# A decoder layer on one core: two row buffers serve first as weight tiles and then as a store for eight more expert results

## The chip, the cores and the metric

The kernel runs on one core of one Trainium2 chip. The metric is the device time of one execution in microseconds (us). Engines are named as in the profile: PE is TensorE's matmul side (PEld its weight loads), DVE is VectorE, ACT is ScalarE, POOL is GpSimd, SP is SyncE, which here only issues DMAs.

## The reference, cut to what matters

One decoder layer over 512 tokens of width 1024, in float32. A token sublayer (retention, forgetting attention, branch gates, projections) is followed by a layer norm. The channel sublayer is where the change lies:

```
def peer(x, w_q, sub_keys, expert_u, expert_v):         # per block of 128 tokens
    q = (xc @ w_q).reshape(n, HEADS, 2, HALF)
    sc = einsum('nhcd,hckd->nhck', q, sub_keys)
    s, idx = top_k(sc, 16)                              # per half key
    cand = s[..., 0, :, None] + s[..., 1, None, :]      # 16 x 16 sums per head
    top_s, pos = top_k(cand, 16);  eid = cid[pos]       # 8 heads x 16 experts of 16384
    gate = softmax(top_s)
    hid = einsum('nhkd,nd->nhk', expert_u[eid], xc)
    act = gelu(hid) * gate
    return einsum('nhk,nhkd->nd', act, expert_v[eid])
h <- LN(alpha*h + peer(h) + sigmoid(h @ W_g + b_g) * (p @ W_ple))
```

## The kernel before, in words

The 512 tokens are two groups of two blocks of 128. Both groups pass through the token sublayer, the first group first. In the channel sublayer they are treated in two ways.

**First group, by gathering.** For each of its two blocks GpSimd gathers 128 rows of `peer_u` and 128 rows of `peer_v` per token partition, one row of 512 KB (128 partitions by 1024 floats) per indirect DMA (`Gather.fetch`, L1081). DVE multiplies a u row with the token and sums it (L1087), and adds a v row, weighted, to the residual (L1097). These 512 row steps run on DVE and in the DMA queues beside everything else, from about 385 us on. Six row buffers (`ROWS`) hold them, and two more (`MORE`) from the beginning of the last stage on.

**Second group, densely.** All 16384 experts are run for its 256 tokens, in 128 steps of 128 experts:
- `up(b)`: eight float32 matmuls of 128x256 (tile `hid`, 16 records in the profile) and a Gelu on ACT into a tile `a`. Weights `ur` come as 1 MB for two steps.
- a gate `gw` per expert and token, which is made from the routing (`select`, on DVE; tile `rt` holds its result) by one-hot products: `by_slot` turns `rt` (matmuls `gt`), DVE writes one-hot tiles `oa` and `ob`, PE multiplies them (`gp`), and ACT copies the products to staging tiles, which go to DRAM (`spread`). There are two spreads, one per block, each 16 pairs of `oa` and `ob`.
- `down(b)`: twelve fp32r matmuls of 128x512 into four PSUM tiles `acc`, from `a` times gate split in high and low parts (`ah`, `al`) and from `peer_v` split likewise (`vh` on ACT, `vl` on DVE).

The gate must be complete before the first `down`, but an `up` needs only the tokens. So 44 ups (`lead`) run early, as filling between other work of PE, and 4 more (`RES`) in the `acc` tiles at the beginning of the last stage. Their results wait in SBUF in the pool `ap`, 50 tiles (`lead + RES + XTRA`). In the last stage the other 80 ups are dealt out between the 128 downs.

**What sets the order.** DVE, POOL and PE run in the order in which the program is written (`in_order`); ACT and SP are ordered by the compiler's scheduler. The written order comes from a planner, `Clock`: it adds estimated times of PE, DVE and the DMA queues. `rows()` puts a row step into DVE's order where the estimate of DVE lies behind that of PE, and `k.fill` puts an up into PE's order, at most 8 at a time, where DVE's estimate is more than 2 us ahead of PE's. Four ups (`RES`) are always left to be issued after the second spread.

**Weight tiles.** `load_raw` (L325) loads projection weights as tiles `wr` of 512 KB into three buffers `wraw` that are used in turn. SP issues the load of a tile when the tile three before it has been used up.

Of the kernel before, what the change touches and what calls it, by code (L numbers as in the profile page):

```python
# [9 lines left out]
F32 = mybir.dt.float32  # L10
# [7 lines left out]
S, D, P = 512, 1024, 128  # L18
# [3 lines left out]
HEADS, K, NK = 8, 16, 128  # L22
# [109 lines left out]
class Clock:  # L132
# [3 lines left out]
    base, more = 0.07, 0.06  # L136
# [72 lines left out]
def setup(ctx, tc, I):  # L209
    k = Ctx()  # L210
    k.clock = Clock()
    nc = Core(tc.nc, k.clock)
    k.nc, k.tc, k.I = nc, tc, I
    k.cp = ctx.enter_context(tc.tile_pool(name="cp", bufs=1))
    k.fp = ctx.enter_context(tc.tile_pool(name="fp", bufs=1))
    k.wp = ctx.enter_context(tc.tile_pool(name="wp", bufs=3))
    k.dr = ctx.enter_context(tc.tile_pool(name="dr", bufs=1, space=DRAM))
    k.tp = None
    k.n = 0
    k.feed, k.side, k.slow, k.fill = Feed(), Feed(), Feed(), Feed()  # L220
    k.later = []

    def flush():

        while k.later:
            f, *a = k.later.pop(0)
            f(*a)

    def rows():
        while k.feed.items and k.clock.row():  # L230
            k.feed.step()

    def tick():
        due, k.later = k.later, []
        for f, *a in due:
            f(*a)
        k.side()
        k.slow()
        k.fill()
        rows()  # L240
    k.tick, k.flush, k.clock.before = tick, flush, rows

    def slot(shape, dt, tag, name):
        pool = k.cp if tag in ("S1", "S2", "S3") else k.q1
        return pool.tile(shape, dt, tag=tag, name=name)
    k.slot = slot

    def uniq(s):
        k.n += 1
        return f"{s}_{k.n}"  # L250
    k.uniq = uniq
    return k
# [71 lines left out]

def load_raw(k, src, c2, g):  # L325

    raw = k.wp.tile([P, 2, 512], F32, tag="wraw", name=k.uniq("wr"))
    k.nc.sync.dma_start(raw, src[g, c2])
    return raw

# [652 lines left out]
ROWS, MORE = 6, 2  # L983
XTRA = 2
RES = 4


class Experts:
# [7 lines left out]
    def up(self, b, ps=None):  # L996
        k, nc, ND = self.k, self.k.nc, self.ND
        if b % 2 == 0:
            self.uraw = k.us.tile([P, 2, 8, P], F32, tag="uraw", name=k.uniq("ur"))
            nc.sync.dma_start(self.uraw, k.I["uT"][b // 2])  # L1000
        if ps is None:
            ps = self.ph.tile([P, ND], F32, tag="hid", name=k.uniq("hid"))
        for c in range(8):
            nc.tensor.matmul(ps, self.uraw[:, b % 2, c, :], k.h1[:, c, :], start=c == 0, stop=c == 7)
        a = self.ap.tile([P, ND], F32, tag="a", bufs=self.lead + RES + XTRA, name=k.uniq("a"))
        nc.scalar.activation(a, ps, AF.Gelu)
        self.act[b] = a

# [91 lines left out]
def channel(k, dense, lead, ctx):  # L1100
    nc, tc, I = k.nc, k.tc, k.I
# [2 lines left out]
    k.us = ctx.enter_context(tc.tile_pool(name="us", bufs=2))  # L1104
    ph = ctx.enter_context(tc.tile_pool(name="ph", bufs=2, space=PSUM))
    ex = Experts(k, dense, gd, lead, ap, ph)
    k.fill.items, k.fill.rate = [(ex.up, b) for b in range(lead)], 8
    k.fill.when = lambda: len(k.fill.items) > RES and k.clock.dve > k.clock.pe + 2
    k.clock.pace, k.clock.due, k.clock.base, k.clock.more = 4.2, k.clock.pe, 0.085, 0.115
    c0 = ExitStack()  # L1110
    with ExitStack() as c1:
        k.pp = c1.enter_context(tc.tile_pool(name="pp2", bufs=4, space=PSUM))
        k.px = c1.enter_context(tc.tile_pool(name="px2", bufs=2, space=PSUM))
        rp = c0.enter_context(tc.tile_pool(name="rp", bufs=2, side="right"))
        routed = [[rp.tile([P, HEADS * K], F32, bufs=1, name=f"rt{n}_{i}") for i in range(3)] for n in range(2)]
        with ExitStack() as c2:
            kp = c2.enter_context(tc.tile_pool(name="kp", bufs=2))
            s16, i16 = product_keys(k, REST, rp, kp, k.h1)
            k.side.items, k.side.rate = [select(k, rp, s16[:, 0], i16[:, 0], *routed[0])], 2.25
            embedding_gate(k, REST, k.h1, kp)  # L1120
            k.side.drain()
        with ExitStack() as c2:
            sps = [c2.enter_context(tc.tile_pool(name=f"sp{i}", bufs=1)) for i in range(2)]
            k.obs = k.slot([P, 2, 8, P], F32, "S2", "ob")
            tabs = k.fp.tile([P, 8, P], F32, tag="xg", bufs=FIRST.nt, name="tabs")
            k.iota = tabs[:, 6, :]
            nc.sync.dma_start(k.iota, I["iota"])
            k.side.items, k.side.rate = [select(k, rp, s16[:, 1], i16[:, 1], *routed[1])], 0.65
            for n in range(len(dense)):
                k.fill()  # L1130
                tr = tabs[:, 3 * n:3 * n + 3, :]
                by_slot(k, tr, routed[n])
                if n == len(dense) - 1:
                    c0.close()
                    dv = ctx.enter_context(tc.tile_pool(name="dv", bufs=2, side="right"))
                    for b in (0, 2):
                        ex.fetch(b, dv)
                for i, _ in enumerate(spread(k, sps, tr, n * P, gd, 4 if n else 8)):
                    k.clock.hold = n == len(dense) - 1 and i >= 28
                    k.tick()  # L1140
                k.side.drain()
            while k.fill.items:
                k.fill.step()
                k.clock.before()
# [3 lines left out]
    po = ctx.enter_context(tc.tile_pool(name="po", bufs=1, space=PSUM))  # L1148
    acc = [[po.tile([P, 512], F32, name=f"acc{m}_{g}") for g in range(2)] for m in range(len(dense))]
    k.tp = dp  # L1150
    k.rows = [(k.gp, "row", ROWS)] * ROWS + [(k.gp, "more", MORE)] * MORE
    k.nrow = 0
    gb = k.slot([P, 2, D], F32, "S2", "gb2")
    g2, b2 = gb[:, 0, :], gb[:, 1, :]
# [8 lines left out]
    for b in range(2):  # L1163
        ex.load(b, dl, dv)
    for i in range(RES):
        ex.up(lead + i, acc[i // 2][i % 2][:, :ex.ND])
# [7 lines left out]
    for b in range(2):  # L1174
        ex.remainder(*ex.act[b])
    done = lead + RES
    for b in range(NK):
        if b + 2 < NK:
            ex.load(b + 2, dl, dv)
        while done < NK and done < lead + RES + (NK - lead - RES) * (b + 1) / (NK - 6):  # L1180
            ex.up(done)
            done += 1
        if b + 3 < NK:
            ex.gate(b + 3, dl, dp)
        k.feed(pace / 2)
        if b + 2 < NK:
            ex.remainder(*ex.vw[b + 2])
        k.feed(pace / 2)
        if b + 2 < NK:
            ex.remainder(*ex.act[b + 2])  # L1190
        if b < NK - 2:
            ex.down(b, acc, range(len(dense)))
        if b == 0:
            for m, t in enumerate(dense):
                for g in range(2):
                    nc.vector.tensor_tensor(acc[m][g], acc[m][g], k.h0[:, t, g * 512:(g + 1) * 512], op=ALU.add)
# [14 lines left out]
def decoder_layer(ctx, tc, I, lead):  # L1211
    k = setup(ctx, tc, I)
# [3 lines left out]
    with ExitStack() as c1:  # L1216
# [16 lines left out]
        k.ws = c2.enter_context(tc.tile_pool(name="ws", bufs=2, side="right"))  # L1233
        act, rq = first_blocks(k, c2.close)
        k.gp = ctx.enter_context(tc.tile_pool(name="gp", bufs=1, side="right"))
        k.rows, k.nrow = [(k.gp, "row", ROWS)], 0
        rp = Borrow(k.tp, c2.enter_context(tc.tile_pool(name="rp0", bufs=2, side="right")))
        h1 = k.slot([P, 8, FIRST.N], F32, "S2", "h1f0")
        in_order = {mybir.EngineType.DVE, mybir.EngineType.Pool, mybir.EngineType.PE}
# [50 lines left out]
```

## Time and profile before

| | |
|---|---|
| median of three runs | 1804.19 us (1802.31 to 1805.01) |
| the profiled execution | 1807.46 us |
| its span, first to last instruction | 1805.3 us |
| PE busy | 1661.7 us, 92% of the span |
| DVE busy | 1378.1 us, 76% |
| moved by DMA | 566.45 MB, 314 GB/s over the span |

The profile is of one execution, about 3 us longer than the median of the others. PE is the busiest engine, but its share is a mean over stages: the chain that ended last passes through PE for about half of the span only. The stages, in us from the beginning of the span: token sublayer of the first group until about 304; routing of the first group and embedding gate until about 398; token sublayer of the second group until about 744; its routing, the early ups and the embedding gate until about 921; a stretch in which PE has almost nothing until 951; the first spread until about 1046 and the second until 1099; eight ups and the first loads of the last stage until 1136; the 128 downs with their ups and with half of all the rows until about 1785; two layer norms and the output.

### The profile page before, as it was taken

What the parts mean: (1) busy time and instruction counts of PE and PEld (TensorE: products, weight loads), DVE (VectorE), ACT (ScalarE), POOL (GpSimd) and SP (SyncE); (2) the same over time, 40 slices, a digit from 0 to 9 for tenths busy, and PEclk for the clock granted to TensorE, in tenths of its full rate; (3) what the DMA queues carried; (4) which work ended last, traced back from release to release, by engine and by line L of the source; (5) the groups of instructions that cost most, each with busy time, mean ns of one, the idle gap of its engine ahead of it and who ended that gap; (6) DMA issues with size and microseconds to landing.
All of it is one profiled execution on the core that took longest, in us unless ns stands there. A gap on an engine that the chain in (4) does not pass through costs nothing.

```text
span 1805.3 us, 22411 instructions
## 1 busy us (share of the span) xinstructions
PE 1661.7 (92%) x7872; PEld 1330.5 (74%) x7872; DVE 1378.1 (76%) x2688; ACT 600.1 (33%) x1098; POOL 633.2 (35%) x524
## 2 busy tenths in 40 slices
PE   6999999998799999799949977999999999999995
PEld 4888996454656886488738966888888788788783
DVE  5654464697778888678988984787788788888888
ACT  4556643221023430111026674332323322332322
POOL 1000000025657555243443301334445444445441
PEclk9999999999899999999979999999999999999998
DMA  8544455879999999788876977999999999999993
GB/s 273 170 138 133 149 162 186 252 259 358 346 328 395 374 349 400 273 331 344 313 274 227 334 255 281 377 390 401 355 414 395 396 409 395 406 396 410 383 378 139
DMA packets 152992, 566.45 MB, mean 314 GB/s; under 512 B 18096, under 2 KB 34992, under 8 KB 134448
## 3 DMA queue, kind: packets, MB, share of 16 engines
q1 hardware_dynamic: 62496, 278.73, 42.0%
q0 software_dynamic: 73872, 269.52, 38.9%
q10 hardware_dynamic: 16512, 16.78, 2.7%
q8 instruction: 62, 1.02, 0.2%
q14 instruction: 50, 0.41, 0.1%
HBM read 543.99 MB, written 20.97 MB: 313 GB/s over the span
## 4 chain that ended last, share of the span: by engine, by line
PE 51%; issue 24%; DVE 10%; DMA 8%; ACT 3%; POOL 3%; SPq 1%; ACTq 0%; DVEq 0%; POOLq 0%
PE hid L194 20%; PE acc L194 17%; PE pj L194 8%; DVE h L1097 4%; DMA row<-in_peer_v,geu 3%; POOL row L1081 2%; PE gp L194 2%; PE lg L194 2%; DMA wr<-in_w_peer_q 2%; DVE s L194 1%; DMA row<-in_peer_u,geu 1%; DVE row L1087 1%; DVE i L194 1%; ACT vh L194 1%; DMA pw<-w 1%
## 5 line engine op out<-in xcount | busy, mean ns | idle before, releaser
L1081 POOL DMA_INDIRECT row<-in_peer_v,geu x256 | 320.5, 1252 | 389.0 <-DVE h L1097 324.7
L194 PE MATMUL hid<-h1f,ur 128*128 128x256 f32 x1984 | 449.9, 381 | 0.0
L1081 POOL DMA_INDIRECT row<-in_peer_u,geu x256 | 301.9, 1179 | 382.6 <-DVE row L1087 244.4
L194 PEld LDWEIGHTS hid<-h1f,ur 128*128 128x128 f32 x1984 | 378.4, 192 | 56.3 <-issue 3.8
L1097 DVE SCALAR_TENSOR_TENSOR h<-row,ghid,h 128x1024 f32<-128x1024 f32 x256 | 327.6, 1280 | 27.2 <-DMA row<-in_peer_v,geu 24.4
L1087 DVE SCALAR_TENSOR_TENSOR row<-row,xg 128x1024 f32<-128x1024 f32 x256 | 308.0, 1217 | 26.0 <-DMA row<-in_peer_u,geu 23.5
L194 DVE TENSOR_TENSOR vl<-vr,vh 128x1024 fp32r<-128x1024 f32 x128 | 156.8, 1226 | 107.5 <-ACT vh L194 107.5
L194 PE MATMUL acc<-vh,al 128*128 128x512 f32 x512 | 203.3, 397 | 21.7 <-DVE al L194 21.6
L194 PE MATMUL acc<-vh,ah 128*128 128x512 f32 x512 | 215.7, 421 | 0.0
L194 PE MATMUL acc<-vl,ah 128*128 128x512 f32 x512 | 201.7, 394 | 1.4 <-DVE vl L194 1.4
L194 DVE TENSOR_TENSOR wl<-wr,wh 128x1024 fp32r<-128x1024 f32 x72 | 88.1, 1223 | 85.9 <-ACT wh L194 85.7
L194 ACT ACTIVATE a<-hid 128x256 f32<-128x256 f32 x124 | 47.4, 382 | 299.9 <-PE hid L194 283.7
L194 ACT ACTIVATE vh<-vr 128x1024 fp32r<-128x1024 f32 x128 | 129.8, 1050 | 20.7 <-PE acc L194 18.9
L194 ACT ACTIVATE ah<-a 128x256 fp32r<-128x256 f32 x128 | 53.1, 416 | 242.3 <-DVE a L194 212.9
L194 PEld LDWEIGHTS acc<-vh,al 128*128 128x128 f32 x512 | 96.6, 189 | 48.9 <-DVE al L194 29.3
L194 PE MATMUL pj<-wr,h1f 128*128 128x512 f32 x256 | 120.7, 613 | 6.6 <-DMA wr<-in_w_peer_q 3.0
L194 PE MATMUL pj<-hT,wr 128*128 128x256 f32 x512 | 117.0, 385 | 0.1
L194 PEld LDWEIGHTS acc<-vl,ah 128*128 128x128 f32 x512 | 97.0, 189 | 24.2 <-DVE vl L194 3.3
L194 PEld LDWEIGHTS acc<-vh,ah 128*128 128x128 f32 x512 | 97.1, 190 | 18.8
L300 POOL TENSOR_TENSOR h<-h,b 128x512 f32<-128x512 f32 x6 | 8.2, 1388 | 291.7 <-ACT h L194 274.4
L194 PEld LDWEIGHTS pj<-hT,wr 128*128 128x128 f32 x512 | 97.3, 193 | 14.0 <-issue 1.4
L194 ACT ACTIVATE wh<-wr 128x1024 fp32r<-128x1024 f32 x72 | 76.2, 1058 | 93.5 <-PE pj L194 76.8
(231 smaller groups left out, 2489.3 us busy)
## 6 DMA issues: line engine op xcount, KB each, us to landing
ur<-in_uT SPq DMA_DIRECT2D x64, 1024.0 KB
vr<-in_vP SPq DMA_DIRECT2D x64, 1024.0 KB
wr<-in_w_in SPq DMA_DIRECT2D x104, 512.0 KB
wr<-in_w_peer_q SPq DMA_DIRECT2D x48, 512.0 KB
gd<-stg ACTq DMA_DIRECT2D x8, 2048.0 KB
gw<-gd SPq DMA_DIRECT2D x15, 1024.0 KB
wr<-in_w_ret_o SPq DMA_DIRECT2D x16, 512.0 KB
wr<-in_w_out SPq DMA_DIRECT2D x16, 512.0 KB
```

The lines of the kernel that those rows point to most:

```text
L194: return f(*a, **kw)
L300: nc.gpsimd.tensor_tensor(dst[:, sl], dst[:, sl], b[:, sl], op=ALU.add)
L1081: k.tc.nc.gpsimd.indirect_dma_start(out=r, out_offset=None, in_=src, in_offset=bass.IndirectOffsetOnAxis(ap=self.e[:, c:c + 1], axis=0))
L1087: self.k.tc.nc.vector.scalar_tensor_tensor(r, r, 1.0, self.x, op0=ALU.mult, op1=ALU.mult, accum_out=self.hid[:, c:c + 1])
L1097: self.k.tc.nc.vector.scalar_tensor_tensor(h1, r, self.hid[:, c:c + 1], h1, op0=ALU.mult, op1=ALU.add)
```

## The change

- **A ring of five.** From the beginning of the second part of the program on (`k.wide`), the second and fourth of every five weight tiles go to the two buffers `more` of the row pool, the other three to `wraw` as before.
- **Eight more results.** `lead` becomes 52. The ups of steps 0 to 7 (`SLAB`) are issued last of the 52, and their results lie in two tiles `slab` of four results each, in the same two buffers `more`, once no more weights come. The pool `ap` stays at 50 tiles.
- **The planner.** Behind the embedding gate DVE's estimate is raised by 20.
- **The last stage.** Rows use only the six buffers `row` until step 8 and then all eight again, and the 72 ups that are left there (80 before) are dealt out from step 6 on.

```
 def load_raw(k, src, c2, g):
+    k.nraw += 1
+    if k.wide and k.nraw % 5 in (2, 4):
+        raw = k.gp.tile([P, 2, 512], F32, tag="more", bufs=MORE, name=k.uniq("wr"))
+    else:
+        raw = k.wp.tile([P, 2, 512], F32, tag="wraw", name=k.uniq("wr"))
...
+SLAB = 8
 class Experts: ... def up(self, b, ps=None):
-        a = self.ap.tile([P, ND], F32, tag="a", bufs=self.lead + RES + XTRA, ...)
+        if b < SLAB:
+            if b % 4 == 0:
+                k.wide = False
+                self.slab = k.gp.tile([P, 4, ND], F32, tag="more", bufs=MORE, ...)
+            a = self.slab[:, b % 4, :]
+        else:
+            a = self.ap.tile([P, ND], F32, tag="a", bufs=self.lead - SLAB + RES + XTRA, ...)
...
-    k.fill.items, k.fill.rate = [(ex.up, b) for b in range(lead)], 8
+    k.fill.items, k.fill.rate = [(ex.up, b) for b in (*range(SLAB, lead), *range(SLAB))], 8
...
             embedding_gate(k, REST, k.h1, kp)
             k.side.drain()
+            k.clock.dve += 20
...
-    k.rows = [(k.gp, "row", ROWS)] * ROWS + [(k.gp, "more", MORE)] * MORE
     for b in range(NK):
+        if b == SLAB:
+            k.rows = [(k.gp, "more", MORE)] * MORE + [(k.gp, "row", ROWS)] * ROWS
+            k.nrow = 0
...
-        while done < NK and done < lead + RES + (NK - lead - RES) * (b + 1) / (NK - 6):
+        while done < NK and done < lead + RES + (NK - lead - RES) * (b - SLAB + 3) / (NK - SLAB - 4):
             ex.up(done)
...
-        decoder_layer(tc, aps, 44)
+        decoder_layer(tc, aps, 44 + SLAB)
```

Where it moves instructions. On SP, the projection for the second group's routing (`wr<-in_w_peer_q`) begins like this before:

```order
L194 DMA wr_5499<-in_w_peer_q 128x1024
L194 DMA keys_5451<-in_keysT 128x512
L194 DMA keys_5535<-in_keysT 128x512
L194 DMA ur_5633<-in_uT 128x2048
L194 DMA ur_5657<-in_uT 128x2048
L194 DMA pw_6141<-pw 128x2x512
L194 DMA bple_6143<-in_b_ple_gate 128x512
L194 DMA wr_5515<-in_w_peer_q 128x1024
```

and like this now:

```order
L194 DMA wr_5499<-in_w_peer_q 128x1024
L194 DMA wr_5515<-in_w_peer_q 128x1024
L194 DMA wr_5539<-in_w_peer_q 128x1024
L194 DMA keys_5451<-in_keysT 128x512
L194 DMA keys_5535<-in_keysT 128x512
L194 DMA ur_5633<-in_uT 128x2048
L194 DMA ur_5657<-in_uT 128x2048
L194 DMA pw_6141<-pw 128x2x512
L194 DMA bple_6143<-in_b_ple_gate 128x512
L194 DMA wr_5572<-in_w_peer_q 128x1024
```

The fourth and fifth weight tile stand ahead of 3.25 MB of other loads; the sixth is now the one behind them.

On PE, between the embedding gate and the first spread (before, then now; each `hid` row is one up):

```order
L194 MATMUL hid_6508<-h1f,ur_6465 128x256 x8
L194 MATMUL hid_6546<-h1f,ur_6544 128x256 x8
L194 MATMUL gt_6557<-ident,rt_0_5440 128x128
L194 MATMUL gt_6557<-ident,rt_1_5441 128x128
L194 MATMUL gt_6557<-ident,rt_2_5442 128x128
L194 MATMUL gp_6572<-oa_6562,ob 128x128 x4
L194 MATMUL hid_6582<-h1f,ur_6544 128x256 x8
L194 MATMUL gp_6596<-oa_6562,ob 128x128 x4
```

```order
L194 MATMUL hid_6546<-h1f,ur_6544 128x256 x8
L194 MATMUL hid_6557<-h1f,ur_6544 128x256 x8
L194 MATMUL hid_6570<-h1f,ur_6568 128x256 x8
L194 MATMUL hid_6581<-h1f,ur_6568 128x256 x8
L194 MATMUL hid_6594<-h1f,ur_6592 128x256 x8
L194 MATMUL hid_6605<-h1f,ur_6592 128x256 x8
L194 MATMUL hid_6618<-h1f,ur_6616 128x256 x8
L194 MATMUL gt_6629<-ident,rt_0_5440 128x128
L194 MATMUL gt_6629<-ident,rt_1_5441 128x128
L194 MATMUL gt_6629<-ident,rt_2_5442 128x128
L194 MATMUL gp_6653<-oa_6634,ob 128x128 x4
L194 MATMUL hid_6663<-h1f,ur_6616 128x256 x8
```

Six of the eight ups now stand ahead of `gt`; of the other two, one is in the first spread (19 ups, 18 before) and one in the second (2, 1 before).

On DVE at the same place, behind the end of the routing (`rt`), before and then now:

```order
L194 TENSOR_TENSOR rt_2_5442<-rt_2_5442,gsm_6530 128x128
L1097 SCALAR_TENSOR_TENSOR h_68<-row_6563,ghid_2841,h_68 128x1024
L194 TENSOR_TENSOR oa_6562<-tabs 128x1024
L194 TENSOR_TENSOR ob<-tabs 128x1024
L194 TENSOR_TENSOR oa_6568<-tabs 128x1024
```

```order
L194 TENSOR_TENSOR rt_2_5442<-rt_2_5442,gsm_6530 128x128
L1109 SCALAR_TENSOR_TENSOR h_68<-row_6635,ghid_2841,h_68 128x1024
L1109 SCALAR_TENSOR_TENSOR h_68<-row_6638,ghid_2841,h_68 128x1024
L1109 SCALAR_TENSOR_TENSOR h_68<-row_6641,ghid_2841,h_68 128x1024
L1109 SCALAR_TENSOR_TENSOR h_68<-row_6644,ghid_2841,h_68 128x1024
L194 TENSOR_TENSOR oa_6634<-tabs 128x1024
```

Three row steps have moved ahead of the first one-hot tile. Over both spreads six row steps have moved out of the last stage (249 are left there, 255 before); ahead of this place DVE's order is the same.

## Rows read from the trace of the kernel before

**Rows 1.** The page's first part: busy us, share of the span, instructions
```profile
PE 1661.7 (92%) x7872; PEld 1330.5 (74%) x7872; DVE 1378.1 (76%) x2688; ACT 600.1 (33%) x1098; POOL 633.2 (35%) x524
```

**Rows 2.** Four stretches: length, busy per engine (count), granted clock, DMA share, GB/s
```profile
921.00:951.00 30.00, 1.95 (x6) 0.72 (x4) 25.30 (x37) 6.72 (x11) 14.79 (x12) 0.58 0.71 258
951.00:1046.00 95.00, 93.96 (x547) 85.82 (x547) 86.47 (x153) 66.30 (x180) 33.88 (x24) 0.97 0.83 297
1046.00:1099.00 53.00, 37.69 (x268) 34.57 (x269) 48.94 (x102) 38.83 (x101) 0.00 (x0) 0.94 0.65 222
1136.00:1760.00 624.00, 609.64 (x2726) 513.53 (x2725) 513.00 (x737) 194.78 (x322) 288.08 (x239) 1.00 0.99 393
```

**Rows 3.** PE's waits, whole span: us in total, times, longest
```profile
PE gt L194 <- DVE rt L194: 25.8, 4, 15.0
...
PE pj L194 <- DMA wr<-in_w_peer_q: 14.3, 8, 11.2
...
PE rs L194 <- DVE sm L194: 11.8, 2, 11.6
```

**Rows 4.** Two moments of the first group's routing: start, us, engine, instruction [idle before]
```profile
326.25 1.98 PE L194 MATMUL pj<-wr,h1f 128*128 128x512 f32 x4 [0.40 <-DMA wr<-in_w_peer_q]
...
348.24 0.29 DVE L194 MAX8 s<-sc 128x8 f32<-128x128 f32 x1 [3.74 <-ACT sc L194]
```

**Rows 5.** SP's issues and PE at the second group's routing
```profile
734.29 7.19 SPq L194 DMA_DIRECT2D wr<-in_w_peer_q  x3
...
748.99 27.68 SPq L194 DMA_DIRECT2D wr<-in_w_peer_q  x5
...
766.10 10.21 PE L194 MATMUL pj<-h1f,wr 128*128 128x256 f32 x32 [11.23 <-DMA wr<-in_w_peer_q]
```

**Rows 6.** Two stretches of 10 us there, columns as in rows 2
```profile
740.00:750.00 10.00, 8.68 (x46) 7.09 (x45) 9.24 (x11) 3.14 (x6) 3.34 (x3) 1.00 0.54 170
750.00:760.00 10.00, 4.86 (x23) 3.95 (x21) 4.06 (x4) 0.00 (x0) 4.45 (x5) 0.93 1.00 383
```

**Rows 7.** DVE there: one row step, the first search, row waits from 744 to 951
```profile
759.58 1.28 DVE L1097 SCALAR_TENSOR_TENSOR h<-row,ghid,h 128x1024 f32<-128x1024 f32 x1 [1.15 <-DMA row<-in_peer_v,geu]
...
777.86 0.30 DVE L194 MAX8 s<-sc 128x8 f32<-128x128 f32 x1 [1.16 <-issue]
...
DVE h L1097 <- DMA row<-in_peer_v,geu: 22.9, 16, 4.8
```

**Rows 8.** PE and DVE ahead of the first spread
```profile
914.51 7.07 PE L194 MATMUL hid<-h1f,ur 128*128 128x256 f32 x32
931.09 0.45 PE L194 MATMUL gt<-ident,rt 128*128 128x128 f32 x1 [9.52 <-DVE rt L194]
946.52 0.47 PE L194 MATMUL gt<-ident,rt 128*128 128x128 f32 x1 [14.98 <-DVE rt L194]
...
947.81 1.28 DVE L1097 SCALAR_TENSOR_TENSOR h<-row,ghid,h 128x1024 f32<-128x1024 f32 x1
...
951.55 2.04 PE L194 MATMUL gp<-oa,ob 128*128 128x128 f32 x8 [3.06 <-DVE ob L194]
```

**Rows 9.** DVE in the second spread: behind its up, and one pair later on
```profile
1057.98 1.23 DVE L194 TENSOR_TENSOR ob<-tabs 128x1024 f32<-128x1024 f32 x1 [3.05 <-PE gp L194]
...
1073.53 0.70 DVE L194 TENSOR_TENSOR oa<-tabs 128x512 f32<-128x512 f32 x1
...
1076.29 0.70 DVE L194 TENSOR_TENSOR oa<-tabs 128x512 f32<-128x512 f32 x1
```

**Rows 10.** The chain that ended last, 1130 to 1170 us: one up, two downs
```profile
1150.58 3.45 PE hid L194 x16
...
1160.22 5.45 PE acc L194 x24
```

**Rows 11.** DVE in the last stage, two steps apart; PE's wait in a double
```profile
1754.69 1.27 DVE L1097 SCALAR_TENSOR_TENSOR h<-row,ghid,h 128x1024 f32<-128x1024 f32 x1
...
1763.53 1.27 DVE L1097 SCALAR_TENSOR_TENSOR h<-row,ghid,h 128x1024 f32<-128x1024 f32 x1
...
1270.04 0.50 PE L194 MATMUL acc<-vh,al 128*128 128x512 f32 x1 [0.98 <-DVE al L194]
```

**Rows 12.** Waits: PE from 1150 to 1760, DVE from 380 to 460
```profile
PE acc L194 <- DVE al L194: 14.3, 15, 1.0
...
DVE row L1087 <- DMA row<-in_peer_u,geu: 8.6, 10, 2.0
```

More of the change, by code (lines that the diff above doesn't have):

```diff
@@ L217, in setup @@
     k.dr = ctx.enter_context(tc.tile_pool(name="dr", bufs=1, space=DRAM))
-    k.tp = None
+    k.tp, k.nraw, k.wide = None, 0, False
     k.n = 0
@@ L325, in load_raw @@
 def load_raw(k, src, c2, g):
-    raw = k.wp.tile([P, 2, 512], F32, tag="wraw", name=k.uniq("wr"))
+    k.nraw += 1
[3 more added lines that the diff above has]
+        raw = k.wp.tile([P, 2, 512], F32, tag="wraw", name=k.uniq("wr"))
     k.nc.sync.dma_start(raw, src[g, c2])
@@ L1004, in up @@
             nc.tensor.matmul(ps, self.uraw[:, b % 2, c, :], k.h1[:, c, :], start=c == 0, stop=c == 7)
-        a = self.ap.tile([P, ND], F32, tag="a", bufs=self.lead + RES + XTRA, name=k.uniq("a"))
+        if b < SLAB:
+            if b % 4 == 0:
+                k.wide = False
+                self.slab = k.gp.tile([P, 4, ND], F32, tag="more", bufs=MORE, name=k.uniq("slab"))
+            a = self.slab[:, b % 4, :]
+        else:
+            a = self.ap.tile([P, ND], F32, tag="a", bufs=self.lead - SLAB + RES + XTRA, name=k.uniq("a"))
         nc.scalar.activation(a, ps, AF.Gelu)
@@ L1235, in decoder_layer @@
         k.gp = ctx.enter_context(tc.tile_pool(name="gp", bufs=1, side="right"))
-        k.rows, k.nrow = [(k.gp, "row", ROWS)], 0
+        k.rows, k.nrow, k.wide = [(k.gp, "row", ROWS)], 0, True
         rp = Borrow(k.tp, c2.enter_context(tc.tile_pool(name="rp0", bufs=2, side="right")))
```

## The prediction

> **What bounds the kernel now.** I read the page's busy shares first, then the stretches, then PE's waits, and last the time lines of the places that the change touches. PE is busy for 92% of the span [rows 1], but no single engine sets the whole of it. In the 128 downs PE works for 609.6 of 624.0 us [rows 2]: that stage is PE's, and its waits are 14.3 us, all for DVE's `al` [rows 12]. In 921 to 951 PE works for 1.95 of 30 us [rows 2]: it waits for `rt`, the end of the routing on DVE (25.8 us in all [rows 3]). In the first spread PE is busy for 93.96 of 95 us, so PE sets it; in the second DVE is busy for 48.94 of 53 us [rows 2], at 2.76 us a pair of one-hot tiles [rows 9], so DVE sets it. An up taken out of the last stage therefore saves PE time there, and what it costs depends on where it goes: nothing in the hole at 921, its full length in the first spread, little in the second.
>
> A second thing is to be seen: from 744 to 951 the path is DVE's, not PE's. PE is stopped for 11.23 us by a weight tile [rows 5], and DVE waits 16 times, 22.9 us in all, for gathered rows [rows 7]; the end of DVE's work there releases `gt`. A weight tile that comes earlier helps the kernel only as far as DVE moves with it.
>
> **The change part by part.** One up is 3.45 us of PE, two downs 5.45, so a down is 2.73 [rows 10].
>
> *Ups out of the last stage.* 8 x 3.45 = **-27.6 us**.
>
> *Six of them into the hole.* PE ended its ups at about 921.5 (914.51 + 7.07) and gets its first one-hot product at 951.55 [rows 8]. 6 x 3.45 = 20.7 us fit into the 30 with room to spare, and `gt` waits for DVE until 946.52 anyway. Cost 0; if each of the three pairs of weights came late by 2 us, still 0. The cover is DVE's routing: were it gone, the 20.7 us would be paid. The granted clock averages 0.58 in the hole [rows 2], so for most of it the clock is at its lower level (1.2 of 2.4 GHz) after PE fell idle, and the first products start slowly. PE will still be idle for some 10 us behind the six ups, so I keep that slow start; it could give back 2 us.
>
> *Three row steps ahead of the first one-hot tile.* They stand on the path that ends the hole: 3 x 1.28 [rows 8] = **+3.8 us**. Their data should be there, since six buffers can be full while DVE finishes the routing.
>
> *One up more in the first spread.* PE sets that stretch, so **+3.5 us** (between 0, if PE had slack that the trace hides, and 3.5).
>
> *One up and one row step more in the second spread.* DVE sets it: the row adds 1.28. The up holds PE, and through the two `ob` buffers DVE: the one that is there now held DVE for 3.05 us [rows 9], with the lower clock in it. The new one comes a pair later, beside the added row. I take 0.6 for it, between 0 and 3.05: **+1.9 us**.
>
> *Steps 0 to 5 without ups.* A step of DVE's takes 4.42 us ((1763.53 - 1754.69) / 2 [rows 11]), a bare down 2.73, so DVE paces them. It has steps 0 to 2 ready ahead and must do three more before down 5 can end, 13.3 us, and add the residual (four tiles of 128x512, at about 0.70 as in [rows 9], 2.8). With 1.1 us from the first product to the first residual and 2.3 for the rest of down 5 that is 19.5, against 6 x 2.73 = 16.4: **+3.1 us**. The bounds are 0 (DVE's lead covers it) and 10.1 (six steps at DVE's pace).
>
> *More doubles.* Two downs behind one up take PE 8.9 us and DVE 8.84: equal. PE waits about 0.98 us [rows 11] in a double whose second `vh` stands behind the up's Gelu on ACT. Counted in ACT's order there are 14 such places among 42 doubles before, which agrees with 14.3 us of waits [rows 12], and 17 among 45 now: **+3 us**, up to +10 if 10 more of the doubles slip. Outside the first six steps PE has (116 x 2.73 + 72 x 3.45) / 116 = 4.87 us a step, still above DVE's 4.42, so PE goes on setting the stage.
>
> *The ring of five.* (a) In the first group's routing PE waits for weights by fractions, as the 0.40 at 326.25; four such waits lie ahead of DVE's last wait for PE at 348.24 [rows 4], about 1.8 us together. From there DVE runs without waiting for PE until PE waits for it (11.6 us for `sm` [rows 3]), so 1.8 us reach 458. (b) Two waits, 1.1 us, in the second group's token sublayer, which is PE's. (c) At 744: the fourth tile was issued at 748.99 behind 3.25 MB of other loads and kept PE until 766.10 [rows 5]. Now the fourth and fifth are issued when places come free, from about 737 on, while the DMA engines are busy for 0.54 [rows 6]; the sixth takes the fourth's place in the queue and will still stop PE for some 4 us. For DVE the gain is the 1.16 us by which its first search waited at 777.86 [rows 7] and up to 2.6 us (1 MB at 383 GB/s) by which its rows are freed. What PE gains beyond that only makes the hole at 921 longer. I take 1.8 + 1.1 + 2.1 = **-5 us**; bounds 0 and -11 (1.8 + 1.1 + 1.2 + 2.6 = 6.7, and a fifth of the 22.9 us of row waits).
>
> The Trainium skill, "DMA: Bandwidth & Descriptors", section "Issuing engines are not separate DMA queues", says that DMAs of all issuing engines run on the same 16 DMA engines and interleave. It speaks against the ring: what weights win, rows lose. The trace agrees where the engines are full (1.00 at 750 to 760, both waits lie there [rows 6, 7]); by the rule alone the ring would give 0, by the 0.54 just before it gives the 2.6 us above.
>
> *Sum.* -27.6 + 3.8 + 3.5 + 1.9 + 3.1 + 3 - 5 = **-17.3 us**, against the profiled execution's own 1807.46 (span 1805.3 and 2.2 around it): 1790.2. That execution lies 3.3 us above the median of the runs, so I take the difference from the median: 1804.2 - 17.3 = **1787 us**.
>
> **Rivals.**
>
> *The ring reaches DVE in full.* Row waits are 22.9 us from 744 on [rows 7]; if a fifth of them and all of (a) to (c) go, the ring gives 11: 1804.2 - 23.3 = 1781. For it: the DMA engines have room until 750. Against: the same bytes still move, only in another order.
>
> *The ring gives nothing, or the last stage is bound by DMA.* Without the 5 us: 1792. The DMA share is 0.99 at 393 GB/s through the downs [rows 2]. If that is a ceiling, the stage shrinks by the bytes that leave it, 8 halves of a weight tile and 6 rows of 128x1024 floats, 14 x 0.524 = 7.3 MB, 18.7 us instead of my 21.5: 1790. Against a ceiling: neither PE nor DVE waits for a DMA in that stage. The same page's section "Where 436 GB/s comes from" lets about 358 GB/s from HBM bind a core; the measured 393 stands above it, so the measurement decides.
>
> *Six row buffers are too few in steps 0 to 7.* With six buffers and full DMA engines a row step took 1.28 + 1.15 us [rows 7]. If that holds for the 16 rows of these steps, DVE needs 6.7 us a step: 6 x (6.7 - 2.73) = 24 us, less 6.9 of two ups and the 3.1 counted, +14: 1801. Against: without ups the stage asks for less (a step's half of `vr`, two rows and an eighth of `gw`, 1.70 MB in 4.42 us, 385 GB/s), and six buffers give each row 13 us to come.
>
> *Slower: the ring starves the gathers.* Two more weight tiles may be in flight beside the rows, and DVE takes rows in order. Its row waits on the path are 8.6 us until 458 and 22.9 from 744 on [rows 12, 7]. If 1 MB more ahead of each burst doubles them, the ring costs 31.5 us instead of giving 5: 1804.2 - 12.3 + 31.5 = 1823. It turns to slower where these waits grow by more than 12.3 us, some 40%. Against: PE uses tiles at the same pace, so a ring of five loads no more in a stretch than one of three, except once at its beginning.
>
> **How the numbers follow.** Forecast 48%, its own range 1783 to 1791; ring in full 14%; ring nothing or DMA-bound 20%; six row buffers 10%; slower 8%. What a measurement of this kernel can tell from no change is about 0.2%, 3.6 us. Faster by more: 48 + 14 + 20 and a third of the 10, 85%; within it 7%; slower 8%. The range leaves out the slower case, most of the six buffers and the end of the full ring: 1777 to 1799.
>
> **What would show it.** In the profile after: no wait of 11 us for `wr<-in_w_peer_q`, a shorter one some 7 us of PE work later; PE busy for about 22 of the 30 us behind the embedding gate; the first one-hot product within a few us of 951; the last `gp` some 4 us later than 1099; 249 rows and 72 ups in the last stage, shorter by some 21 us, with small gaps of PE between the first downs. I am wrong if PE's waits for `al` pass 30 us, if DVE begins to wait for rows in steps 0 to 8, or if its row waits ahead of 951 grow.

## The result and the profile after

| | before | after |
|---|---|---|
| median of the runs taken side by side | 1806.7 us | 1795.8 us |
| ratio, 95% interval | | 0.9942 [0.9933, 0.9951] |
| the profiled execution, its span | 1807.46, 1805.3 us | 1795.69, 1793.6 us |

The change wins 0.58%, 10.5 us. Forecast were 17.3 us (a ratio of 0.9904): the direction is right, but 7 us of the gain are missing. Taken from the prediction's base of 1804.2 the measured time is 1793.7 us: inside the whole range (1777 to 1799), outside the forecast's own (1783 to 1791). The busy shares hardly move, as PE does the same work in a shorter span [rows 1]. The page's first part of the kernel after:

```profile
PE 1658.9 (92%) x7872; PEld 1329.8 (74%) x7872; DVE 1377.3 (77%) x2688; ACT 603.5 (34%) x1100; POOL 631.4 (35%) x524
```

ACT has 1100 instructions where it had 1098: remember the two. The stretches that answer to [rows 2] come next; the columns are the same.

```profile
921.00:951.00 30.00, 17.78 (x81) 14.83 (x79) 26.65 (x37) 7.07 (x11) 16.64 (x14) 0.85 0.90 345
959.00:1056.00 97.00, 96.45 (x561) 88.11 (x562) 87.24 (x154) 65.69 (x179) 36.66 (x26) 0.98 0.85 306
1056.00:1111.00 55.00, 42.22 (x293) 38.87 (x292) 51.97 (x111) 40.81 (x104) 0.94 (x1) 0.94 0.71 247
1146.00:1749.00 603.00, 584.40 (x2603) 489.11 (x2602) 506.29 (x727) 192.97 (x315) 283.60 (x237) 1.00 1.00 395
```

The hole is filled: PE works for 17.78 us of the 30 that had 1.95 (forecast were about 22). The first spread is PE's as before (96.45 of 97), the second DVE's (51.97 of 55). PE's waits over the whole span, for [rows 3, 12]:

```profile
PE acc L194 <- DVE al L194: 25.8, 25, 2.4
...
PE gp L194 <- DVE ob L194: 12.6, 3, 7.0
PE rs L194 <- DVE sm L194: 12.5, 1, 12.5
PE gt L194 <- DVE rt L194: 11.9, 3, 10.3
...
PE lg L194 <- ACT l L194: 3.8, 3, 1.7
...
PE pj L194 <- DMA wr<-in_w_peer_q: 2.9, 1, 2.9
```

The wait for `rt` has gone from 25.8 to 11.9 and that for `w_peer_q` from 14.3 to 2.9, as the change means to do. One line is new: `lg` waits for ACT's `l`, 3.8 us. It belongs to a place that the prediction did not look at.

Measured between landmarks of PE's order, which the change leaves in place, the span's 11.7 us come out so (times of the landmark before and after, from PE's time line):

| from, to | before | after | difference |
|---|---|---|---|
| start, first logits `lg` of the second group (535.66, 529.94) | 535.66 | 529.94 | -5.7 |
| to the first transpose of `z` (653.59, 655.61) | 117.93 | 125.67 | **+7.7** |
| to the first transpose of `h` (740.97, 742.24) | 87.38 | 86.63 | -0.8 |
| to the last `gt` of the first spread (948.04, 951.73) | 207.07 | 209.49 | +2.4 |
| to the first one-hot product (951.55, 959.16) | 3.51 | 7.43 | +3.9 |
| to `gt` of the second spread (1044.83, 1055.94) | 93.28 | 96.78 | +3.5 |
| to the end of the last `gp` (1099.64, 1111.03) | 54.81 | 55.09 | +0.3 |
| to the end of the span (1805.3, 1793.6) | 705.7 | 682.6 | -23.1 |

The last four rows are near to the steps of the prediction. The first four are not: the ring wins far more than was thought by 530, all of it is gone by 656, and the second routing takes 2.4 us more where 2.1 less were forecast. The forgetting attention of the second group, 118 us that PE works through without a stop before, takes 126.

**Where it goes.** Two moments of PE in the kernel after:

```profile
538.35 0.55 PE L194 MATMUL lg<-ident,l 128*128 128x128 f32 x3 [1.53 <-ACT l L194]
538.73 5.29 PE L194 MATMUL pj<-wr,hT 128*128 128x512 f32 x8
...
590.22 0.89 PE L194 MATMUL lg<-ident,l 128*128 128x128 f32 x4 [1.75 <-ACT l L194]
590.91 1.38 PE L194 MATMUL py<-fv,l 128*128 128x64 f32 x6
592.08 4.59 PE L194 MATMUL pj<-hT,wr 128*128 128x256 f32 x16
```

Two more such waits follow, 0.50 for `l` at 614.28 and, behind the landmark, 1.05 for `zT` at 658.13. And behind the first two the matmuls run slower: the eight records at 538.73 take 5.29 us, and eight such records in the kernel before 3.70 (at 532.53). The granted clock fell at the same time. Stretches of 5 us in the kernel after, columns as above:

```profile
540.00:545.00 5.00, 5.00 (x13) 2.27 (x11) 3.85 (x8) 0.78 (x2) 3.27 (x4) 0.73 0.99 376
545.00:550.00 5.00, 5.00 (x21) 3.00 (x21) 4.66 (x9) 3.16 (x6) 4.09 (x4) 1.00 0.98 371
590.00:595.00 5.00, 4.78 (x20) 4.29 (x21) 3.98 (x8) 1.33 (x5) 4.09 (x4) 0.66 1.02 410
595.00:600.00 5.00, 5.00 (x29) 4.03 (x28) 1.73 (x7) 1.19 (x4) 2.15 (x2) 1.00 0.96 357
```

0.73 and 0.66 mean that the clock was at the lower of its two levels (1.2 of 2.4 GHz) for part of the stretch, each time after PE had been idle. What held `l` up at 590 is seen on ACT, first after, then before, at the same branch gate:

```profile
583.44 1.28 ACT L194 ACT_TABLE_LOAD   x1
586.37 1.70 ACT L194 ACTIVATE sgr<-pj,bbg 128x256 f32<-128x256 f32 x4 [1.65 <-PE pj L194]
588.09 1.28 ACT L194 ACT_TABLE_LOAD   x1
589.39 0.69 ACT L194 ACTIVATE l<-lg,mx 128x512 f32<-128x512 f32 x1
```

```profile
588.95 0.69 ACT L194 ACTIVATE l<-lg,mx 128x512 f32<-128x512 f32 x1 [3.23 <-DVE mx L194]
589.53 0.19 ACT L194 ACTIVATION_READ_ACCUMULATOR l<-lg,mx 128x1 f32 x1
589.74 1.28 ACT L194 ACT_TABLE_LOAD   x1
591.04 1.57 ACT L194 ACTIVATE sgr<-pj,bbg 128x256 f32<-128x256 f32 x4
```

Before, the exponential of this tile (`l<-lg,mx`) comes first and the sigmoids (`sgr`) follow it. After, the sigmoids stand ahead: ACT loads their table, waits 1.65 us for PE's `pj`, does them, loads the table of the exponential again, and only then makes the `l` for which PE stands still. At the next gate the sigmoids are split in two, with the exponential between them: these are the two instructions more, both table loads (48, before 46). Nobody wrote this order. DVE, POOL and PE keep the written order, ACT and SP are left to the compiler's scheduler, and it laid ACT out anew when the weight tiles were given other buffers. The Trainium skill, "ScalarE: Activation LUTs", section "What ACT_TABLE_LOAD costs", gives about 1283 ns for the load, as the trace does, and about 1380 ns more for a drain. Here the exponential starts at 589.39, 1.30 us after the load began: no drain is seen, and the trace decides.

The wait at 538 is another. There ACT's order is as before, and its exponential waits for the maximum `mx` from DVE. After, then before:

```profile
537.03 0.55 DVE L194 TENSOR_REDUCE mx<-lg 128x1 f32<-128x384 f32 x1
537.62 0.58 ACT L194 ACTIVATE l<-lg,mx 128x384 f32<-128x384 f32 x1 [12.05 <-DVE mx L194]
```

```profile
539.93 0.55 DVE L194 TENSOR_REDUCE mx<-lg 128x1 f32<-128x384 f32 x1
540.51 0.58 ACT L194 ACTIVATE l<-lg,mx 128x384 f32<-128x384 f32 x1 [9.95 <-DVE mx L194]
```

`mx` comes 7.1 us behind the first logits (529.94), before 4.3 (535.66). Four row steps stand ahead of it on DVE. Their waits for gathered rows, after (525 to 537) and before (530 to 540):

```profile
DVE row L1099 <- DMA row<-in_peer_u,geu: 6.6, 4, 2.9
```

```profile
DVE row L1087 <- DMA row<-in_peer_u,geu: 4.5, 4, 1.8
```

By the starts of the logits, 3.4 of the 7.7 us are lost here (from the first to the third, 13.52 us instead of 10.09), 3.6 at the gate of 590 (9.46 instead of 5.86) and 0.7 at that of 614 (6.95 instead of 6.25). So in this execution ACT's new order accounts for 4.3 us of the 7.7, and the wait behind late rows on DVE, with the lower clock after it, for 3.4.

**Second routing.** PE there, for [rows 5], then DVE's row waits, for [rows 7]:

```profile
745.51 17.53 PE L194 MATMUL pj<-h1f,wr 128*128 128x256 f32 x80 [1.32 <-ACT h1f L194]
762.88 1.95 PE L194 MATMUL sp<-keys,qs 128*128 128x128 f32 x16
767.75 4.54 PE L194 MATMUL pj<-h1f,wr 128*128 128x256 f32 x12 [2.93 <-DMA wr<-in_w_peer_q]
```

```profile
DVE h L1109 <- DMA row<-in_peer_v,geu: 26.6, 19, 5.8
```

The stop of 11.23 us is now 2.93, two tiles later, and of no use: DVE, which sets this stretch, waits 26.6 us for rows instead of 22.9.

**Ahead of the first spread.** PE and DVE, for [rows 8]:

```profile
936.08 3.69 PE L194 MATMUL hid<-h1f,ur 128*128 128x256 f32 x16 [1.58 <-DMA ur<-in_uT]
939.61 0.27 PE L194 MATMUL gt<-ident,rt 128*128 128x128 f32 x1
950.21 0.47 PE L194 MATMUL gt<-ident,rt 128*128 128x128 f32 x1 [10.33 <-DVE rt L194]
...
959.16 2.04 PE L194 MATMUL gp<-oa,ob 128*128 128x128 f32 x8 [6.98 <-DVE ob L194]
```

```profile
951.50 5.24 DVE L1109 SCALAR_TENSOR_TENSOR h<-row,ghid,h 128x1024 f32<-128x1024 f32 x4
```

The six ups end at about 939.6 and cost nothing: DVE's `rt` comes 10 us later. The cover is thin where DVE is sooner: in ups_alone and ring_early below PE waits 2.9 and 1.3 us for `rt` there. Then four row steps instead of one stand in front of the one-hot tiles, and PE waits 6.98 us for `ob` instead of 3.06.

### The profile page after: what moved, and what is told of

Same layout as the page of the kernel before. It is cut to its first block, busy times and chain, and to the rows that moved or that the text cites. A ratio compares the mean times of both kernels' runs of the same rounds, so it can differ in the third digit from the quotient of the medians.

```text
span 1793.6 us, 22415 instructions
## 1 busy us (share of the span) xinstructions
PE 1658.9 (92%) x7872; PEld 1329.8 (74%) x7872; DVE 1377.3 (77%) x2688; ACT 603.5 (34%) x1100; POOL 631.4 (35%) x524
## 4 chain that ended last, share of the span: by engine, by line
PE 48%; issue 21%; DVE 16%; DMA 8%; ACT 4%; POOL 2%; SPq 1%; ACTq 0%; DVEq 0%; POOLq 0%
PE acc L194 16%; PE hid L194 15%; PE pj L194 12%; DVE h L1109 4%; DMA row<-in_peer_v,geu 2%; DVE row L1099 1%; DVE s L194 1%; DMA wr<-in_w_peer_q 1%; POOL row L1093 1%; PE lg L194 1%; DVE i L194 1%; DMA row<-in_peer_u,geu 1%; PE gp L194 1%; DMA ur<-in_uT 1%; ACT vh L194 1%
## 5 line engine op out<-in xcount | busy, mean ns | idle before, releaser
L1093 POOL DMA_INDIRECT row<-in_peer_v,geu x256 | 313.9, 1226 | 389.2 <-DVE h L1109 315.7
L1093 POOL DMA_INDIRECT row<-in_peer_u,geu x256 | 306.7, 1198 | 377.4 <-DVE row L1099 229.5
L194 PE MATMUL acc<-vh,al 128*128 128x512 f32 x512 | 204.0, 398 | 25.9 <-DVE al L194 25.8
```

The source lines that it names most:

```text
L194: return f(*a, **kw)
L1093: k.tc.nc.gpsimd.indirect_dma_start(out=r, out_offset=None, in_=src, in_offset=bass.IndirectOffsetOnAxis(ap=self.e[:, c:c + 1], axis=0))
```

## The experiments

All times are medians of runs taken beside the kernel before, on the same chip; the ratio is to it. "Attention" is the stretch from the first logits to the first transpose of `z`, as in the table above.

**1 to 4: the two halves apart, and the ring in parts.** *ring_alone* adds to the kernel before only the ring (`k.wide` stays on, `lead` 44). *ups_alone* is the changed kernel with

```
-        k.rows, k.nrow, k.wide = [(k.gp, "row", ROWS)], 0, True
+        k.rows, k.nrow = [(k.gp, "row", ROWS)], 0
```

*ring_early* is the changed kernel with the first line here, *ring_gap* with both:

```
+        k.wide = False
         last_blocks(k, act, rq, h1)
+        k.wide = True
```

Expected of ring_alone:

> The kernel before with the ring of five weight tiles alone; 44 ups kept as before, the row order of before. TensorE's and VectorE's orders are those of before, ScalarE's order around the second group's forgetting attention is that of the changed kernel. Theory A (the traces): the ring wins 5 to 6 us up to the logits at 530, ScalarE's new order gives 7 back by 660 (TensorE waits for l at about 538 and 590), and the weight tiles that start earlier hold up the rows of the second routing by some 3 us more: in all between -1 and +4 us. Theory B (the prediction's sum): -5 us. Theory C (the order of ScalarE harmless, the loss of 530 to 660 a matter of the slab's program alone): -6 to -8 us, and no waits for l.

Expected of ups_alone:

> The changed kernel with the ring left at three tiles; the eight more ups, the row order and the 20 us put on VectorE's clock kept. TensorE's and VectorE's orders are those of the changed kernel, ScalarE's order around the second group's attention is that of before. Theory A: the ups alone win at least what the whole change wins: -11 to -14 us, with row waits of 744 to 951 at 23 us and the 11 us wait for w_peer_q back. Theory B (the prediction's sum without its 5 us for the ring): -12.3 us. Theory C (the ring does win and the ups win less than their 27.6 less 15.3): -4 to -7 us.

Expected of ring_early:

> The changed kernel with the ring of five switched back to three where the second group's attention begins, and left there. TensorE's and VectorE's orders are those of the changed kernel, ScalarE's around the second group's attention is that of before. Theory A (ScalarE's order makes the loss of 530 to 660): the 5 us won by 458 stay until 744, the waits for l are gone: -15 to -18 us against before, some 5 us faster than the changed kernel. Theory C (the ring's earlier loads or something else makes the loss): like the changed kernel, -10 to -12 us, and 740 is reached no earlier than in the kernel before.

Expected of ring_gap:

> As ring_early, but the ring of five switched on again for the second group's routing. TensorE's and VectorE's orders are those of the changed kernel, the second group's attention loads through three tiles as in ring_early, but ScalarE's order there is that of the changed kernel. Theory A: the loss of 530 to 660 is back (waits for l at 538 and 590 us, lower granted clock): -9 to -12 us against before, as the changed kernel. Theory C (the loss comes of the ring of five in that attention): as ring_early up to 744, -15 to -18 us.

| | median | ratio, interval | attention | row waits, 744 to 959 |
|---|---|---|---|---|
| ring_alone | 1807.7 | 0.9999 [0.9986, 1.0011] | 121.3 us | 25.6 us |
| ups_alone | 1795.5 | 0.9935 [0.9914, 0.9957] | 117.9 | 20.9 |
| ring_early | 1786.7 | 0.9893 [0.9873, 0.9913] | 118.2 | 20.0 |
| ring_gap | 1798.9 | 0.9948 [0.9928, 0.9967] | 123.9 | 29.0 |

The ring alone gives nothing, and the ups alone give what the whole change gives (0.65%, 11.7 us). ring_early, with the ring switched off from the second group's attention on, is some 9 us faster than the changed kernel. Where ACT keeps its old order (before, ups_alone, ring_early) the attention takes 118 us; where it has the new one (after, ring_alone, ring_gap) it takes 121 to 126, although in ring_gap the tiles of that attention come through a ring of three. PE's waits there in ring_alone:

```profile
PE lg L194 <- ACT l L194: 2.8, 3, 1.7
...
PE tr L194 <- ACT zT L194: 1.1, 1, 1.1
```

The 2.8 us for `l` are most of the 3.4 that ring_alone loses (the wait for `zT` comes behind the first transpose of `z`); its granted clock averages 1.00. 0.6 of the 2.8 are again a wait behind DVE's `mx`, at 542. ring_gap waits 2.3 us for `l`, at the two gates alone, has 10 us at a clock of 0.80 (593 to 603) and loses 6.0. So at the two gates the new order costs 2.6, 4.3 and 5.9 us in the three profiles that have it (ring_alone, after, ring_gap): 2.3 us of waiting in each, and more where the clock fell. The wait behind `mx` does not need the new order: early_no20 below, with the old one, waits 0.74 us for `l` at 542.92, behind a row wait of DVE of 2.69, and its attention takes 119.2 us. What ring_gap changes against ring_early, the loads for the second routing, comes only after the work that the scheduler reorders.

**5: ACT in written order.** *act_written* is the changed kernel with ACT, too, kept in order through that attention (`not parts` is the second group; the lines below the first are only indented):

```
+    with (k.tc.manual_schedule(engines={mybir.EngineType.Activation}) if not parts else ExitStack()):
         side.items, side.rate = [forgetting_attention(k, G, fq, yf)], 18 / 23
         swish(k, G, z, act)
         ...
         side.drain()
         k.flush()
```

> The changed kernel with ScalarE, too, kept in written order through the second group's forgetting attention and branch gates; the sigmoids of a branch gate stay together there, with 47 table loads in the program instead of 49. Theory A (ScalarE's order, not the ring's traffic, makes the loss of 530 to 660): the waits for l at 590 and 614 are gone, and the stretch from the first logits to the first transpose of z falls from 125.7 to some 118 to 121 us: 3 to 8 us faster than the changed kernel, -14 to -18 against before, and still slower than ring_early, whose second routing has fewer row waits. Theory C (the ring's traffic there): the stretch stays above 123, no gain.

1787.8 us, 0.9905 [0.9889, 0.9920]. The attention takes 118.3 us, and PE waits 0.2 us for `l` in it:

```profile
580.00:590.00 10.00, 10.00 (x58) 8.81 (x58) 8.19 (x17) 2.98 (x7) 6.70 (x6) 1.00 1.02 411
590.00:600.00 10.00, 10.00 (x53) 8.41 (x52) 8.65 (x25) 5.58 (x10) 5.71 (x6) 1.00 1.03 406
```

With the whole ring in place and nothing changed but ACT's order, 6.7 us are back (3.4 to 9.9 by the two intervals). Of these the traces show the 4.3 at the two gates and the 1.05 for `zT`, which is gone too. The long wait behind `mx` is not in this profile either (0.16 us are left, at 542.74), though nothing here orders DVE or the rows otherwise; how many executions of the changed kernel have it is not known.

**6: the same order without the change.** *before_act* puts those lines into the kernel before.

> The kernel before, unchanged but for ScalarE's written order in the second group's forgetting attention and branch gates, as in act_written. Theory A (the written order only mends what the compiler's new order spoilt): within 1.5 us of before, ratio 0.9992 to 1.0008, the stretch from the first logits to the first transpose of z stays at 118 us. Rival (the written order is better in itself, so act_written says nothing on the loss): 4 to 8 us faster than before.

1807.3 us, 1.0011 [0.9997, 1.0025], the attention 117.9 us. The written order is no better than the compiler's old one. It only undoes the new one, so act_written tells of the loss and not of a gain of its own.

**7: the ring in the first routing alone.** *ring_first* is ring_alone with `k.wide = False` ahead of `last_blocks`.

> The kernel before with the ring of five in the first group's routing and embedding gate alone, three tiles again from the second group's attention on; 44 ups. The orders of TensorE and VectorE are those of before, ScalarE's in the second group's attention too. Theory A (the ring's gain lies in the first routing, where VectorE's waits for the scores sc fell from 22.7 to 18.6 us, and was lost again by ScalarE's order and the rows): 4 to 5 us faster than before, ratio 0.9970 to 0.9980. The prediction's step (a) alone: 1.8 us, 0.9990. If the ring gives nothing anywhere: 1.0000.

1801.3 us, 0.9975 [0.9960, 0.9991]: 4.5 us (1.6 to 7.2). DVE's waits for the scores in the first group's routing, from 300 to 460, before and then in ring_first:

```profile
DVE s L194 <- ACT sc L194: 22.7, 4, 13.5
```

```profile
DVE s L194 <- ACT sc L194: 18.8, 4, 11.7
```

Every kernel with the ring there shows 18.6 to 18.8, and those without it (before, before_act, ups_alone) 22.1 to 23.1.

**8: the ring in the second routing.** *early_act* is ring_early with ACT in written order, so act_written without the ring from the attention on.

> ring_early with ScalarE's written order as in act_written, so it differs from act_written only in the ring, which has three tiles again from the second group's attention on. Theory A (the ring of five costs in the second routing what its weight tiles take from the rows): VectorE's row waits of 744 to 951 some 2 to 4 us shorter than in act_written, 2 to 4 us faster, about -20 against before. Theory E (the ring is harmless there once ScalarE's order is mended): as act_written, 0.990 to 0.991.

1788.1 us, 0.9912 [0.9898, 0.9926], against 0.9905 [0.9889, 0.9920] of act_written. No difference can be told; row waits are 21.5 and 22.6 us. My theory expected 2 to 4 us and is not borne out. The profiles with the ring in the second routing have row waits of 22.6 to 29.0 us and those without 20.0 to 23.0, so the rows may lose a little, but one profile each does not show a price.

**9: no rows ahead of the first one-hot tile.** *early_hold* is ring_early with

```
+                k.clock.hold = n == 0
                 by_slot(k, tr, routed[n])
```

> ring_early with row steps held back from the first by_slot until the first two pairs of one-hot tiles are written; four row steps move from there into the first spread and behind it. Theory P (the prediction's step: rows ahead of the first one-hot tile stand on the path, 1.28 us each): the wait of the first gp for ob falls from 7.1 to some 3 us and the first gp comes 4 to 5 us earlier; as TensorE sets the first spread, that holds: 4 us faster than ring_early, about -23 against before. Theory R (the rows come back on the path later, as VectorE sets the second spread): the same start of the first spread, and a later end of the second; within 1 us of ring_early.

1782.1 us, 0.9863 [0.9846, 0.9880]: 0.3% less than ring_early (5.4 us, 0.7 to 10 by the two intervals). First ring_early, then early_hold, PE at the first product:

```profile
949.68 1.62 PE L194 MATMUL gp<-oa,ob 128*128 128x128 f32 x6 [7.13 <-DVE ob L194]
```

```profile
948.53 1.83 PE L194 MATMUL gp<-oa,ob 128*128 128x128 f32 x7 [3.06 <-DVE ob L194]
```

4.07 us of wait are gone, as expected. But the first product comes only 1.15 us sooner, as the routing's end (`rt`) came 2.9 us later in this execution, the first spread takes 98.0 us instead of 96.1, and 3.5 of the 3.8 us between the two profiles lie behind the last `gp`. So the step on the path is shown by the wait, and where the 5.4 us come from is not. With hold_rows8 below this is the fastest of the kernels.

**10: the hole left empty.** *early_no20* is ring_early without `k.clock.dve += 20`.

> ring_early without the 20 us put on VectorE's clock ahead of the hole: the planner then leaves the hole behind the embedding gate short of some six ups, and puts them between the one-hot products. Theory P (six ups in the hole cost nothing, an up in the first spread its full 3.45 us, three rows ahead of the one-hot tile 3.9): 6 x 3.45 - 3.9 = 17 us slower than ring_early, so about -2 against before, with the wait for rt back at some 20 us or more. Theory Q (the lower clock behind an idle TensorE makes up a good part, so the hole was not free): slower by under 10 us.

1792.8 us, 0.9925 [0.9913, 0.9937]: 5.8 us slower than ring_early (1.6 to 10), not 17. In the profiles six ups leave the hole (21 instead of 27 up to 945), PE waits for `rt` again (25.2 us), and they, with one of the first spread, land in the second, not in the first as both theories had it. There DVE sets the pace and PE has idle time, so from the second `gt` to the end of the last `gp` it takes 18.6 us more, not 20.7. Against that the first product comes 2.1 us sooner behind the first transpose of `h`, an up fewer stands in the first spread (2.9), and 3.6 us come back in the last stage. Neither expectation was right in its reason; the hole is the better place by some 6 us.

**11: eight row buffers in the second routing.** *early_rows8* is ring_early with

```
         k.wide = False
+        k.rows, k.nrow = [(k.gp, "row", ROWS)] * ROWS + [(k.gp, "more", MORE)] * MORE, 0
         last_blocks(k, act, rq, h1)
```

and `k.rows` back to `row` when up 0 takes the slab.

> ring_early with the two buffers given to the gathered rows, eight buffers in all, from the second group's attention until the slab takes them. TensorE's and VectorE's orders are those of ring_early. Theory A (VectorE sets 744 to 951, and its waits for rows are for buffers): two more rows lie ready at the beginning of each burst, row waits of 744 to 951 fall from 20 to some 10 us, and the first spread starts 5 to 10 us earlier, so 4 to 9 us faster than ring_early. Theory D (the DMA engines are full in those bursts, so more buffers bring nothing): row waits stay within 3 us of 20, same time.

1783.7 us, 0.9878 [0.9860, 0.9896], against 0.9893 of ring_early: the intervals overlap. DVE's row waits from 744 to 951:

```profile
DVE h L1110 <- DMA row<-in_peer_v,geu: 9.5, 10, 1.4
```

They halve (20.0 in ring_early), and the first product comes 206.2 us after the first transpose of `h` instead of 211.7. So these waits are for buffers, and not only for DMA engines that are full, as I had read [rows 6, 7]. A further gain would meet PE, which now sets the end of the hole: it reaches `gt` at 943.1 and finds all of `rt` there. In the profile 2.5 of the 5.5 us are lost again ahead of the first transpose of `h` (740.45, in ring_early 737.95); the runs tell 2.7 us (-2.2 to 7.6), which is not told from nothing.

**12: both.** *hold_rows8* is early_hold with early_rows8.

> early_hold and early_rows8 together: ring of five in the first routing only, the two buffers then for the gathered rows until the slab takes them, no rows ahead of the first one-hot tiles. If the two gains add: -28 against before (1779 where before is 1807). If both only shorten the same wait ahead of the first spread, which TensorE's ups then bound: as early_hold, -23 to -25.

1781.6 us, 0.9868 [0.9853, 0.9883], as early_hold: the two do not add. That both shorten the same wait, with PE's ups behind it, fits the profile (all three `gt` at 947.17 without a wait, then 3.07 us for `ob`).

## Why the prediction was right in direction and 7 us too good

| step of the prediction | forecast | measured |
|---|---|---|
| last stage: eight ups less, steps 0 to 5, more doubles | -27.6 + 3.1 + 3 = -21.5 | -23.1 from the last `gp` on |
| six ups into the hole | 0 | 0: `rt` comes 10.3 us after them |
| three rows ahead of the one-hot tile | +3.8 | +3.9; held back, -4.1 of that wait |
| an up more in the first spread | +3.5 | +3.5 |
| an up and a row more in the second spread | +1.9 | +0.3 |
| all of the ups | -12.3 | -11.7 (ups_alone, -15.5 to -7.8) |
| ring (a), first routing | -1.8 | -4.5 (ring_first, -7.2 to -1.6) |
| ring (b), second group's token sublayer | -1.1 | both waits gone, ahead of the first logits; then **+7.7 - 0.8**: 4.3 by ACT's new order, 3.4 by late rows |
| ring (c), second routing | -2.1 | +2.4 in the profile; not told from 0 by the runs (act_written, early_act) |
| the ring in sum | -5 | 0 (ring_alone), or -5 with ACT's order mended (0.9935 to 0.9905; -10 to -1) |

**The step that failed** is "two waits, 1.1 us, in the second group's token sublayer, which is PE's". The prediction looked there for waits that the ring takes away and for nothing that it could bring. The sublayer was PE's only because ACT delivered each `l` in time, which hangs on ACT's order, and that is the compiler's, and on DVE's `mx`, which stands behind rows. ACT's order had moved, and the two table loads more stand in the changed program's order for everyone to see without a run. The prediction speaks of that order at one place alone, the doubles of the last stage. Undoing that one thing (act_written) gives 0.9905, and the control (before_act) excludes that the written order is simply better: that ACT's order cost the missing time, or at least 3.4 us of it, is shown. That 0.9905 meets the 0.9904 of the forecast is in part luck: (a) gave 4.5 us instead of 1.8, (c) nothing that can be told instead of 2.1, and the last stage and the second spread each came out 1.6 us better in the profile.

**Mis-sized.** Step (a) counted 1.8 us from four waits of PE for weights ahead of 348. DVE waits less for the scores over the whole routing, 4.1 us. PE's waits for weights from 300 to 460 were seven, 3.0 us in all, and every one is gone; what the rest of the 4.1 is was not tried. Step (c) was mostly a gain on PE that DVE, the engine on the path, did not need; its part for DVE is below what a run can tell. The second spread took less than thought: the up and the row there cost 0.3 us together.

**The rivals.** "The ring gives nothing, 1792" is nearest in the time, though not by its reason: DMA did not bind the last stage, which shrank by 23.1 us, and not by the 18.7 of the bytes, with the engines at 395 GB/s. The rule of the Trainium skill ("DMA: Bandwidth & Descriptors", section "Issuing engines are not separate DMA queues") that DMAs of all issuers interleave on the same engines, which the prediction set against the ring, does not decide either. In the first routing weights won 4 us of DVE's waits for scores, while its row waits there (380 to 460) are 7.1 to 10.6 us in the kernels with the ring and 8.6 to 10.8 without. Ring in full, six row buffers and starved gathers are out. The signs that I named: PE's waits for `al` stay below 30 us (25.8); but DVE does wait for rows behind step 0 (2.9 us, twice, before 1200, which costs PE 1.5 us for `al`), and row waits ahead of 951 did grow, by 5.0 us of the 12.3 that would have turned the sign. The first product came at 959 and not "within a few us of 951", and the last `gp` 11 us later instead of 4: mostly through the 7.7 us that were lost at 530 to 656 and the 2.4 of the second routing.

Of the loss it stays open whether the late rows at 525 to 537 come of the ring or of the one execution (act_written and ring_alone, with the ring there, wait 4.7 and 4.6 us at that place). It stays open, too, which of the ring's loads makes the compiler choose anew: the order flips in ring_gap and not in ring_early, which differ only in loads that the program issues later. Why the clock fell behind some of the waits and not behind others was not tried.

## What to carry to other kernels

Where some engines are ordered by hand and others by a scheduler, a change of a load's time can reorder the others at a place that it does not touch: compare every engine's order, and the count of table loads, before pricing the change. A stage is "PE's" only as long as each engine that feeds it keeps its place; list the tiles it gets from the scheduled engines and what could come to stand ahead of them. And a resource that wins in one stage need not be left on in the next: the same two buffers as weight tiles in the first routing, with rows held back from the path later on, gave 0.9863 where the change gave 0.9942.

## What the runs showed of the hardware

A wait of less than 2 us can cost more than its length on PE. After 1.53 and 1.75 us of idle time the granted clock was 0.73 (540 to 545) and 0.66 (590 to 595), and eight matmul records took 5.29 us instead of 3.70. How far it falls is not fixed: at the same instruction, after the same wait of 1.75 us, ring_gap has 0.53 from 590 to 595 and ring_alone stays at 1.00. The other thing is the rate of DMA: 395 GB/s over 603 us at a share of 1.00, in which PE waited for no DMA and DVE once, 1.9 us.
